# Sums of squares and gate products moved from GpSimd to VectorE, a fixed order behind the mixer's norm, and state pieces in another order, in one layer of a streaming encoder

## The chip, the cores and the metric

The kernel runs on one core of one Trainium2 chip. The metric is the device time of one execution in microseconds (us). A core has engines that run their own instruction streams beside each other: TensorE (PE, matmuls; PEld is its weight load), VectorE (DVE), ScalarE (ACT), GpSimd (POOL) and SyncE (SP), whose stream here only issues DMA transfers. A stream is carried out in order; between engines the instructions wait on semaphores. SBUF is the on-chip memory with 128 partitions, PSUM the memory into which TensorE accumulates.

## The reference

One layer of an encoder, for 256 rows of a new stream (prompt) and 32 rows of a running one (sample), 288 rows in all, that share the weights. What bears on this case:

```
xn    = rmsnorm(x, norm_mix_pre)
proj  = xn @ w_in                    # 2048 -> u_pool 1024 | z 2048 | xBC 2560 | dt 32
pool  = pool_mixer(u_pool)           # trailing means over 2/4/8/16 rows, minus u, @ w_pool, scaled
ssd   = ssd_mixer(z, xBC, dt)        # scan, times silu(z), then an rmsnorm in each of 2 groups of 1024
mix   = concat[pool, ssd] @ w_out    # 3072 -> 2048
x     = x + rmsnorm(mix, norm_mix_post)
hn    = rmsnorm(x, norm_ffn_pre)
up    = causal_dwconv(hn @ w_up)     # 2048 -> 2 x 5632
x     = x + rmsnorm((silu(gate) * value) @ w_down, norm_ffn_post)
```

with `rmsnorm(x, g) = x / sqrt(mean(x^2) + 1e-6) * g`. Besides the rows of both streams the layer returns new histories and the new scan state of each stream (`new_ssd_p`, `new_ssd_s`): for the prompt the sum over its rows of B times the decayed x, for the sample the same sum plus the decayed old state.

## The kernel before

**Layout.** Activations lie with the model's dimension on the partitions, as tiles of 128 x 288 floats. 2048 dimensions are 16 tiles (`KD`). A product with weights keeps float32 accuracy by a split: each operand is a high part (`fp32r`, made by ScalarE with a copy) and a low part (the rest, made by VectorE), and `mm3` (L135 to L138) issues three matmuls for each pair of tiles: high weight by high activation (L136), high weight by low activation (L137), low weight by high activation (L138). Weights come by DMA as `raw` tiles and are split into `whi` (L130 or L788, ScalarE) and `wlo` (L131 or L789, VectorE); `raw`, `whi` and `wlo` have 4 buffers each, so a split can run at most four ahead of TensorE. Activations are split by `split_from` (L92 to L102).

**What sets the order.** The code is written in program order, and a scheduler orders each engine's stream by its own estimate of readiness. `tc.high_priority(offset=...)` lets it take an instruction earlier. `tc.keep_in_program_order` and `tc.issue_after(x)` bind an instruction behind others of its engine. PSUM tiles come from two pools: `acc` with 5 buffers and `aux` with 3, which serves short sums (`psum_m`, `psum_t`) and further accumulators (`acc_x`).

**The stage of w_in's end and the pool mixer (L571 to L654).** `xs` are the 16 tiles of the scan's output, times silu(z). The norm of a group of 8 tiles gives a factor `rg[0]` or `rg[1]`. Tiles 0 to 7 are multiplied by `rg[0]` on VectorE earlier (L562); tiles 8 to 15 by `rg[1]` on GpSimd (L640), two for each of four turns of the loop over pool groups. That loop takes the last columns of w_in (`pool_in`), builds trailing sums `win` on VectorE (L610), forms `dpool` (L616, L617) and splits it into `du` (high part L95), which TensorE takes for w_pool. Behind it the loop over `NX` (L645) splits all `xs` into `mixs`, the inputs of w_out.

**w_out (L656 to L743).** `project` goes through 16 output tiles; for each, `mix_out` (L662) squares the result for the norm and copies it into `mg`, the `x1` tile, on ScalarE. The squares of the first 14 are summed on GpSimd into `msum`, the last two stay apart as `msq`. The mean over the partitions is three matmuls into `psum_m`: of `msum`, and of each `msq`. Between the output tiles stand four pieces of the scan state. `state_in(j)` (L681) loads `sx` (x) and `sh` (old sample state) by GpSimd's DMA queue, 2 buffers each, and decays them on VectorE (L694, L696); `state_p(j)` (L699) makes the prompt's state `pst` and `state_s(j)` (L709) the sample's `psts`, to which GpSimd adds `sh` (L716). Pieces 0 and 1 are done inside w_out, pieces 2 and 3 are held back to the end, where TensorE would wait for the norm.

**Behind the mixer's norm (L746 to L797).** `root` (L236) makes `rm`, the reciprocal root, with a ScalarE and a VectorE instruction. Then for each of 16 tiles k: VectorE multiplies `mg` by `rm` (L758) and adds the old x from `xT` (L759); ScalarE makes the high part of `hn` (L770) and VectorE the low part (L771); ScalarE squares the tile, GpSimd adds the square to `xsum` (L780); ScalarE and VectorE split the weights of this k for 7 output tiles of w_up (L788, L789); TensorE does 7 x 3 matmuls. The mean of `xsum` (`psum_t`, L797) gives the factor `r2`, by which the outputs of w_up are multiplied when they leave PSUM. From k = 2 on a weight split is bound behind both parts of `hn` of its tile.

Of the kernel before, what the change touches and what calls it, by code (L numbers as in the profile page):

```python
# [43 lines left out]
def body(  # L44
# [590 lines left out]
    for n, i in enumerate((3, 2, 1, 0)):  # L635
        ps = ups.pop() if n == 0 else project(win, [(256 * i, 256)], xn, K16)
        for j in range(2):
            pool_in(2 * i + j, ps[j])
        for t in range(8 + 2 * n, 10 + 2 * n):
            pool.tensor_tensor(xs[t], xs[t], rg[1], op=ALU.mult)  # L640
        if n:
            pool_tile(2 * i + 2)
            pool_tile(2 * i + 3)
            pool_group(i + 1)
    for t in range(NX):  # L645
        a = atile("mixs")
        split_from(a, xs[t], g_ssd[:, t : t + 1])
        mix[NU + t] = a
        if t == 3:
            pool_tile(0)  # L650
            pool_tile(1)
# [7 lines left out]
    def mix_out(p_):  # L659
        m = len(x1)  # L660
        o = btile("mg")
        if m < KD - 2:  # L662
            sq_add(msum, p_, op_, m == 0)
        else:
            q = msq[m - KD + 2]
            with tc.high_priority(offset=400):
                act.activation(q, p_, AF.Square)
            last_sq.append(q)
        if m == KD - 2:
            pe.matmul(p_m, mean, q, start=False, stop=False)  # L670
        act.activation(o, p_, AF.Copy, scale=g_mix_post[:, m : m + 1])
        x1.append(o)
# [36 lines left out]
    def state_s(j, x, h, pin=False):  # L709
# [4 lines left out]
        ho = stp[0].tile([P, 512], F32, tag="ho", bufs=2, name="hos")  # L714
        act.activation(ho, st, AF.Copy)
        pool.tensor_tensor(ho, ho, h, op=ALU.add)  # L716
        sp.dma_start(out=new_ssd_s[:, 512 * j : 512 * j + 512], in_=ho)
# [27 lines left out]

    state_s(3, *late_in[3], pin=True)  # L746
    tc.keep_in_program_order(pe.matmul(p_m, mean, last_sq[1], start=False, stop=True))
    state_p(3, *late_in[3], pin=True)
    state_s(2, *late_in[2], pin=True)
    state_p(2, *late_in[2], pin=True)  # L750
    rm = const.tile([P, NT], F32, tag="spread", bufs=3, name="rm")
    tc.keep_in_program_order(root(rm, p_m))
    hn = []
    up1 = [(aux([P, NT], "acc_x") if m in (3, 4) else acc_ps.tile([P, NT], F32, tag="acc", name="acc")) for m in range(7)]
    raws = {}

    def residual(t):
        tc.keep_in_program_order(dve.tensor_tensor(x1[t], x1[t], rm, op=ALU.mult))  # L758
        tc.keep_in_program_order(dve.tensor_tensor(x1[t], x1[t], xT[:, t, :], op=ALU.add))  # L759

    residual(0)
    for k in range(KD):
        if k % 2 == 0:
            raw = wpool.tile([P, 2, 896], F32, tag="raw", name="raw")
            with tc.high_priority(offset=ahead[0]):
                sp.dma_start(out=raw, in_=w_up1[:, k : k + 2, :])
        if k + 1 < KD:
            residual(k + 1)
        a = atile("hn")
        hi = act.activation(a[:, 0, :], x1[k], AF.Copy, scale=g_ffn_pre[:, k : k + 1])  # L770
        lo = dve.scalar_tensor_tensor(  # L771
            a[:, 1, :], x1[k], g_ffn_pre[:, k : k + 1], a[:, 0, :].bitcast(F32), op0=ALU.mult, op1=ALU.subtract
        )
        tc.keep_in_program_order(lo)
        if k == 0:
            act.activation(xsum, x1[k], AF.Square)
        else:
            q = op_.tile([P, NT], F32, tag="sq", bufs=2, name="sq")
            act.activation(q, x1[k], AF.Square)
            pool.tensor_tensor(xsum, xsum, q, op=ALU.add)  # L780
        hn.append(a)
        whi, wlo = wtile("hi", 1, 896)[:, 0, :], wtile("lo", 1, 896)[:, 0, :]
        with ExitStack() as order:
            order.enter_context(tc.high_priority(offset=ahead[0]))
            if k > 1:
# [4 lines left out]
        for m in range(7):  # L790
            c = slice(m * P, (m + 1) * P)
            mm3(up1[m], whi[:, c], wlo[:, c], a, k == 0, k == KD - 1)
            if k == KD - 1 and m == 1:
                p_ = aux([P, NT], "psum_t")
                r2 = const.tile([P, NT], F32, tag="spread", bufs=3, name="r2")
                with tc.high_priority(offset=1000):
                    pe.matmul(p_, mean, xsum, start=True, stop=True)  # L797
                    root(r2, p_)
# [39 lines left out]
    def up(kind, j, view=None):  # L838
# [4 lines left out]
        project(*((view, [(0, P)]) if view is not None else (wuv, [(kind * (D_FF - 512) + j * P - 512, 256)])), hn, K16, done=out)  # L843
# [277 lines left out]
```

## Time and profile before

| | |
|---|---|
| three runs | 1338.0, 1338.72, 1338.82 us; median 1338.72 |
| the profiled execution | 1337.7 us |
| its span | 1336.0 us |
| granted TensorE clock, mean | 0.996 |
| bytes moved by DMA | 249.82 MB |
| HBM over the span | 186 GB/s |

A row of a group reads: line of the code, engine, operation, output<-inputs, shapes, how many; busy us and mean ns of one; idle time of the engine just before and what ended it. A row of the timeline reads: start in us from the span's start, duration in us, engine, line, operation, tiles, how many together, and in brackets the idle time before it with what ended it. TensorE's instructions overlap: the starts, not the durations, tell its pace. A row of the windows reads: the stretch, its length, busy us and count for PE, PEld, DVE, ACT and POOL, then the granted TensorE clock (1.00 is full), the DMA share and GB/s.

### The profile page before, as it was taken

What the parts mean: (1) busy time and instruction counts of PE and PEld (TensorE: products, weight loads), DVE (VectorE), ACT (ScalarE), POOL (GpSimd) and SP (SyncE); (2) the same over time, 40 slices, a digit from 0 to 9 for tenths busy, and PEclk for the clock granted to TensorE, in tenths of its full rate; (3) what the DMA queues carried; (4) which work ended last, traced back from release to release, by engine and by line L of the source; (5) the groups of instructions that cost most, each with busy time, mean ns of one, the idle gap of its engine ahead of it and who ended that gap; (6) DMA issues with size and microseconds to landing.
All of it is one profiled execution on the core that took longest, in us unless ns stands there. A gap on an engine that the chain in (4) does not pass through costs nothing.

```text
span 1336.0 us, 25101 instructions
## 1 busy us (share of the span) xinstructions
PE 1312.7 (98%) x10041; PEld 1297.0 (97%) x10041; DVE 887.1 (66%) x1437; ACT 665.3 (50%) x1002; POOL 239.8 (18%) x376
## 2 busy tenths in 40 slices
PE   7999999999999999999999999999999999999996
PEld 7999999999999989999999999999999999999996
DVE  7898998788544469977676644335666666664444
ACT  7558777446443455644445433334454444454442
POOL 6221102240212123211121100001111111101110
PEclk9999999999999999999999999999999999999998
DMA  7667884456656435766544544554544544566653
GB/s 285 230 194 258 280 248 150 152 207 216 238 205 205 146 121 189 208 180 187 179 158 164 176 146 170 174 182 159 181 166 158 174 174 158 168 239 175 208 177 94
DMA packets 104009, 249.82 MB, mean 187 GB/s; under 512 B 63748, under 2 KB 69444, under 8 KB 81492
## 3 DMA queue, kind: packets, MB, share of 16 engines
q1 hardware_dynamic: 101972, 243.11, 55.4%
q0 software_dynamic: 1488, 4.92, 1.1%
q8 instruction: 78, 1.28, 0.4%
q14 instruction: 39, 0.32, 0.1%
q10 hardware_dynamic: 432, 0.19, 0.1%
HBM read 236.23 MB, written 11.95 MB: 186 GB/s over the span
## 4 chain that ended last, share of the span: by engine, by line
PE 91%; DVE 3%; DMA 2%; issue 1%; POOL 1%; ACT 0%; SPq 0%; DVEq 0%; POOLq 0%; ACTq 0%
PE acc L138 30%; PE acc L136 29%; PE acc L137 29%; DMA xw<-xs_d 1%; POOL xs L640 1%; DMA raw<-in_w_first 1%; DVE xn L100 1%; PE py L467 1%; DMA xs_d<-blocks 1%; DVE wlo L271 0%; DVE xr L959 0%; PE acc_x L138 0%; PE run_a L1002 0%; PE acc_x L137 0%; DVE wlo L131 0%
## 5 line engine op out<-in xcount | busy, mean ns | idle before, releaser
L131 DVE TENSOR_TENSOR wlo<-raw,whi 128x1024 fp32r<-128x1024 f32 (+1 forms) x386 | 464.3, 1204 | 329.4 <-ACT whi L130 328.7
L130 ACT ACTIVATE whi<-raw 128x1024 fp32r<-128x1024 f32 (+1 forms) x386 | 399.3, 1036 | 471.9 <-PE acc L137 384.9
L138 PE MATMUL acc<-hn,wlo 128*128 128x288 f32 x1376 | 409.3, 298 | 0.0
L136 PE MATMUL acc<-hn,whi 128*128 128x288 f32 x1376 | 402.5, 293 | 0.5 <-ACT hn L770 0.5
L137 PE MATMUL acc<-hn,whi 128*128 128x288 f32 x1376 | 399.6, 291 | 1.2 <-DVE hn L771 1.2
L137 PEld LDWEIGHTS acc<-hn,whi 128*128 128x128 f32 x1376 | 258.9, 188 | 1.5 <-DVE hn L771 1.4
L136 PEld LDWEIGHTS acc<-hn,whi 128*128 128x128 f32 x1376 | 258.7, 188 | 1.3 <-ACT hn L770 1.3
L138 PEld LDWEIGHTS acc<-hn,wlo 128*128 128x128 f32 x1376 | 258.7, 188 | 0.0
L136 PE MATMUL acc<-xn,whi 128*128 128x288 f32 x688 | 203.8, 298 | 5.6 <-ACT whi L270 5.6
L137 PE MATMUL acc<-xn,whi 128*128 128x288 f32 x688 | 200.8, 293 | 0.0
L138 PE MATMUL acc<-xn,wlo 128*128 128x288 f32 x688 | 198.7, 298 | 1.6 <-DVE wlo L271 1.4
L138 PE MATMUL acc<-fa,wlo 128*128 128x288 f32 x660 | 196.4, 298 | 0.0
L136 PE MATMUL acc<-fa,whi 128*128 128x288 f32 x660 | 193.1, 293 | 0.0
L137 PE MATMUL acc<-fa,whi 128*128 128x288 f32 x660 | 191.4, 290 | 0.0
L136 PEld LDWEIGHTS acc<-xn,whi 128*128 128x128 f32 x688 | 130.3, 189 | 6.5 <-ACT whi L270 5.6
L137 PEld LDWEIGHTS acc<-xn,whi 128*128 128x128 f32 x688 | 130.3, 189 | 0.2
L138 PEld LDWEIGHTS acc<-xn,wlo 128*128 128x128 f32 x688 | 127.7, 189 | 2.6 <-DVE wlo L271 1.6
L137 PEld LDWEIGHTS acc<-fa,whi 128*128 128x128 f32 x660 | 123.9, 188 | 0.0
L136 PEld LDWEIGHTS acc<-fa,whi 128*128 128x128 f32 x660 | 123.9, 188 | 0.0
L138 PEld LDWEIGHTS acc<-fa,wlo 128*128 128x128 f32 x660 | 123.9, 188 | 0.0
L816 POOL COPY fc_stage<-ebuf 128x4 f32<-128x4 f32 x88 | 27.2, 309 | 466.8 <-DVE ebuf L815 466.8
L812 POOL COPY ebuf<-pf 128x2 f32<-128x2 f32 x88 | 67.4, 767 | 140.6 <-DVE fc L822 79.4
(279 smaller groups left out, 1716.1 us busy)
## 6 DMA issues: line engine op xcount, KB each, us to landing
raw<-in_w_up SPq DMA_DIRECT2D x80, 1024.0 KB, 4.8
raw<-in_w_in SPq DMA_DIRECT2D x38, 1024.0 KB, 5.4
raw<-in_w_down SPq DMA_DIRECT2D x32, 1024.0 KB, 4.8
raw<-in_w_out SPq DMA_DIRECT2D x24, 1024.0 KB, 4.8
raw<-in_w_down SPq DMA_DIRECT2D x16, 768.0 KB, 4.3
raw<-in_w_up SPq DMA_DIRECT2D x8, 896.0 KB, 4.5
gb<-g_d SPq DMA_DIRECT2D x8, 832.0 KB, 6.6
raw<-in_w_first SPq DMA_DIRECT2D x7, 768.0 KB, 10.2
```

Source lines behind the costliest of these rows:

```text
L100: dve.scalar_tensor_tensor(a[:, 1, :], src, scale, a[:, 0, :].bitcast(F32), op0=ALU.mult, op1=ALU.subtract),
L130: act.activation(hi, raw[:, k : k + n, :], AF.Copy)
L131: dve.tensor_tensor(lo, raw[:, k : k + n, :], hi.bitcast(F32), op=ALU.subtract)
L136: pe.matmul(out, wh, a[:, 0, :], start=start, stop=False)
L137: pe.matmul(out, wh, a[:, 1, :], start=False, stop=False)
L138: pe.matmul(out, wl, a[:, 0, :], start=False, stop=stop)
L467: pe.matmul(y[:, 0:256], xw[:, 0, c], m[:, j, 0:256], start=True, stop=False)
L640: pool.tensor_tensor(xs[t], xs[t], rg[1], op=ALU.mult)
L812: pool.tensor_copy(e[:, 258:260], pf[:, 4:6, i])
L816: pool.tensor_copy(fc_stage[:, :, :, i], e[:, 256:324].rearrange("p (s c) -> p s c", c=34)[:, :, 0:2])
```

## The change

It has five parts.

1. The products of `xs` 8 to 15 with `rg[1]` move from GpSimd (L640) to VectorE, into the loop that splits `xs`; each stands behind the low part of the tile before it.
2. Both matmuls of `msq` into `psum_m` are issued together right behind the last matmul of w_out, then both sample pieces and then both prompt pieces of the state. Before, the first was issued in `mix_out`, and the order behind it was sample piece 3, last sum, prompt 3, sample 2, prompt 2.
3. `in_line` binds VectorE's instructions behind the norm (product, addition, low part, sum of squares) each to the one before it, in program order. The product and addition of tile k + 1 stand ahead of the low part of tile k. The sum of squares moves from GpSimd to this line. Weight splits are bound behind `hn` from k = 4 on, not from k = 2.
4. `psum_t` is allocated ahead of the 7 accumulators, in the buffer that follows `psum_m`'s in turn, its matmul is bound in place (in the last tile, behind the second of 7 outputs), and the product of w_up that comes next takes its accumulator from the `aux` pool (`spare=1`).
5. `state_s` copies the sum into `sx`, and GpSimd adds it into `sh`, which is written out; the tile `hos` goes.

```diff
--- before.py
+++ after.py
@@ -636,15 +636,16 @@
         ps = ups.pop() if n == 0 else project(win, [(256 * i, 256)], xn, K16)
         for j in range(2):
             pool_in(2 * i + j, ps[j])
-        for t in range(8 + 2 * n, 10 + 2 * n):
-            pool.tensor_tensor(xs[t], xs[t], rg[1], op=ALU.mult)
         if n:
             pool_tile(2 * i + 2)
             pool_tile(2 * i + 3)
             pool_group(i + 1)
     for t in range(NX):
         a = atile("mixs")
-        split_from(a, xs[t], g_ssd[:, t : t + 1])
+        if t >= 8:
+            with tc.issue_after(low.ins):
+                dve.tensor_tensor(xs[t], xs[t], rg[1], op=ALU.mult)
+        _, low = split_from(a, xs[t], g_ssd[:, t : t + 1])
         mix[NU + t] = a
         if t == 3:
             pool_tile(0)
@@ -666,8 +667,6 @@
             with tc.high_priority(offset=400):
                 act.activation(q, p_, AF.Square)
             last_sq.append(q)
-        if m == KD - 2:
-            pe.matmul(p_m, mean, q, start=False, stop=False)
         act.activation(o, p_, AF.Copy, scale=g_mix_post[:, m : m + 1])
         x1.append(o)
 
@@ -711,10 +710,9 @@
         ins = pe.matmul(st, btok[:, j // 2, 2, :], x[:, 2, :], start=True, stop=True)
         if pin:
             tc.keep_in_program_order(ins)
-        ho = stp[0].tile([P, 512], F32, tag="ho", bufs=2, name="hos")
-        act.activation(ho, st, AF.Copy)
-        pool.tensor_tensor(ho, ho, h, op=ALU.add)
-        sp.dma_start(out=new_ssd_s[:, 512 * j : 512 * j + 512], in_=ho)
+        act.activation(x[:, 2, :], st, AF.Copy)
+        pool.tensor_tensor(h, h, x[:, 2, :], op=ALU.add)
+        sp.dma_start(out=new_ssd_s[:, 512 * j : 512 * j + 512], in_=h)
 
     late_in = {}
 
@@ -743,20 +741,32 @@
             act.dma_start(out=new_pool, in_=np_stage)
 
 
+    for i in range(2):
+        tc.keep_in_program_order(pe.matmul(p_m, mean, last_sq[i], start=False, stop=i == 1))
     state_s(3, *late_in[3], pin=True)
-    tc.keep_in_program_order(pe.matmul(p_m, mean, last_sq[1], start=False, stop=True))
+    state_s(2, *late_in[2], pin=True)
     state_p(3, *late_in[3], pin=True)
-    state_s(2, *late_in[2], pin=True)
     state_p(2, *late_in[2], pin=True)
     rm = const.tile([P, NT], F32, tag="spread", bufs=3, name="rm")
-    tc.keep_in_program_order(root(rm, p_m))
+    root(rm, p_m)
+    out_temp = lambda: op_.tile([P, NT], F32, tag="sq", bufs=2, name="sq")
     hn = []
+    p_t = aux([P, NT], "psum_t")
     up1 = [(aux([P, NT], "acc_x") if m in (3, 4) else acc_ps.tile([P, NT], F32, tag="acc", name="acc")) for m in range(7)]
     raws = {}
 
+    line = []
+
+    def in_line(f, *args, **kw):
+        with ExitStack() as order:
+            if line:
+                order.enter_context(tc.issue_after(line[-1].ins))
+            line.append(f(*args, **kw))
+        return line[-1]
+
     def residual(t):
-        tc.keep_in_program_order(dve.tensor_tensor(x1[t], x1[t], rm, op=ALU.mult))
-        tc.keep_in_program_order(dve.tensor_tensor(x1[t], x1[t], xT[:, t, :], op=ALU.add))
+        in_line(dve.tensor_tensor, x1[t], x1[t], rm, op=ALU.mult)
+        in_line(dve.tensor_tensor, x1[t], x1[t], xT[:, t, :], op=ALU.add)
 
     residual(0)
     for k in range(KD):
@@ -764,25 +774,25 @@
             raw = wpool.tile([P, 2, 896], F32, tag="raw", name="raw")
             with tc.high_priority(offset=ahead[0]):
                 sp.dma_start(out=raw, in_=w_up1[:, k : k + 2, :])
+        a = atile("hn")
+        hi = act.activation(a[:, 0, :], x1[k], AF.Copy, scale=g_ffn_pre[:, k : k + 1])
         if k + 1 < KD:
             residual(k + 1)
-        a = atile("hn")
-        hi = act.activation(a[:, 0, :], x1[k], AF.Copy, scale=g_ffn_pre[:, k : k + 1])
-        lo = dve.scalar_tensor_tensor(
-            a[:, 1, :], x1[k], g_ffn_pre[:, k : k + 1], a[:, 0, :].bitcast(F32), op0=ALU.mult, op1=ALU.subtract
+        lo = in_line(
+            dve.scalar_tensor_tensor,
+            a[:, 1, :], x1[k], g_ffn_pre[:, k : k + 1], a[:, 0, :].bitcast(F32), op0=ALU.mult, op1=ALU.subtract,
         )
-        tc.keep_in_program_order(lo)
         if k == 0:
             act.activation(xsum, x1[k], AF.Square)
         else:
-            q = op_.tile([P, NT], F32, tag="sq", bufs=2, name="sq")
+            q = out_temp()
             act.activation(q, x1[k], AF.Square)
-            pool.tensor_tensor(xsum, xsum, q, op=ALU.add)
+            in_line(dve.tensor_tensor, xsum, xsum, q, op=ALU.add)
         hn.append(a)
         whi, wlo = wtile("hi", 1, 896)[:, 0, :], wtile("lo", 1, 896)[:, 0, :]
         with ExitStack() as order:
             order.enter_context(tc.high_priority(offset=ahead[0]))
-            if k > 1:
+            if k > 3:
                 order.enter_context(tc.issue_after(hi.ins))
                 order.enter_context(tc.issue_after(lo.ins))
             act.activation(whi, raw[:, k % 2, :], AF.Copy)
@@ -791,11 +801,10 @@
             c = slice(m * P, (m + 1) * P)
             mm3(up1[m], whi[:, c], wlo[:, c], a, k == 0, k == KD - 1)
             if k == KD - 1 and m == 1:
-                p_ = aux([P, NT], "psum_t")
                 r2 = const.tile([P, NT], F32, tag="spread", bufs=3, name="r2")
                 with tc.high_priority(offset=1000):
-                    pe.matmul(p_, mean, xsum, start=True, stop=True)
-                    root(r2, p_)
+                    tc.keep_in_program_order(pe.matmul(p_t, mean, xsum, start=True, stop=True))
+                    root(r2, p_t)
     x1d = dram.tile([NT, D_MODEL], F32, name="x1d")
     outp.close()
 
@@ -840,7 +849,10 @@
         def out(m, p_):
             conv_[kind, j + m] = fconv(kind * NF + j + m, p_)
 
-        project(*((view, [(0, P)]) if view is not None else (wuv, [(kind * (D_FF - 512) + j * P - 512, 256)])), hn, K16, done=out)
+        if view is not None:
+            project(view, [(0, P)], hn, K16, done=out, spare=1)
+        else:
+            project(wuv, [(kind * (D_FF - 512) + j * P - 512, 256)], hn, K16, done=out)
 
     def up_half(lo_, hi_):
         for j in range(lo_, hi_, 2):
```

How the instructions move is shown at three places. First, GpSimd in the stage of the pool mixer, both kernels in one piece (`ubuf` are the pool inputs, `np_stage` the new pool history):

```order
 L604 COPY np_stage<-ubuf_3587 128x30
 L604 COPY np_stage<-ubuf_3589 128x30
-L640 TENSOR_TENSOR xs<-xs,rg 128x288 x7
 L599 COPY ubuf_3587<-pc 128x15
-L640 TENSOR_TENSOR xs<-xs,rg 128x288
 L599 COPY ubuf_3589<-pc 128x15
 L604 COPY np_stage<-ubuf_3591 128x30
```

The eight products are gone, and the copies into the `ubuf` tiles follow each other. On VectorE, in the same stage, the first of them stand here (`du` low part of a pool input, `mixs` low part of an `xs` tile):

```order
 L131 TENSOR_TENSOR wlo<-raw,whi 128x1024
 L100 TENSOR_SCALAR mixs<-xs,g_ssd,mixs 128x288
+L647 TENSOR_TENSOR xs<-xs,rg 128x288
 L96 TENSOR_TENSOR du<-dpool,du 128x288
-L100 TENSOR_SCALAR mixs<-xs,g_ssd,mixs 128x288 x3
 L131 TENSOR_TENSOR wlo<-raw,whi 128x1024
 L597 TENSOR_TENSOR ubuf_3591<-acc,rstd 128x256
 L598 TENSOR_TENSOR ubuf_3591<-acc,rstd 128x32
-L100 TENSOR_SCALAR mixs<-xs,g_ssd,mixs 128x288 x3
+L100 TENSOR_SCALAR mixs<-xs,g_ssd,mixs 128x288
+L647 TENSOR_TENSOR xs<-xs,rg 128x288
```

The products stand one by one ahead of the low parts of their tiles, behind the low part of the tile before.

Second, ScalarE at the end of w_out, before (`msq` squares of the last two outputs, `whi` weight splits, L788 those of w_up, `rm` the root, `ho` and `hos` copies of the state):

```order
L788 ACTIVATE whi<-raw 128x896 x2
L667 ACTIVATE msq_3581<-acc 128x288
L671 ACTIVATE mg<-acc,par_119 128x288
L667 ACTIVATE msq_3582<-acc 128x288
L671 ACTIVATE mg<-acc,par_119 128x288
L715 ACTIVATE hos<-psts 128x512
L237 ACTIVATE rm<-psum_m,eps_t 128x288
L706 ACTIVATE ho<-pst 128x512
L715 ACTIVATE hos<-psts 128x512
L770 ACTIVATE hn<-mg,par_119 128x288
L776 ACTIVATE xsum<-mg 128x288
L706 ACTIVATE ho<-pst 128x512
```

and now:

```order
L798 ACTIVATE whi<-raw 128x896 x3
L668 ACTIVATE msq_3581<-acc 128x288
L670 ACTIVATE mg<-acc,par_119 128x288
L798 ACTIVATE whi<-raw 128x896
L668 ACTIVATE msq_3582<-acc 128x288
L670 ACTIVATE mg<-acc,par_119 128x288
L237 ACTIVATE rm<-psum_m,eps_t 128x288
L713 ACTIVATE sx<-psts 128x512 x2
L705 ACTIVATE ho<-pst 128x512
L778 ACTIVATE hn<-mg,par_119 128x288
L786 ACTIVATE xsum<-mg 128x288
L778 ACTIVATE hn<-mg,par_119 128x288
```

One weight split more stands ahead of the squares, one between them, and the root comes before all copies of the state.

Third, VectorE behind the reciprocal, before (`mg` the products and additions, `hn` low parts, `wlo` weight splits):

```order
L789 TENSOR_TENSOR wlo<-raw,whi 128x896 x2
L238 RECIPROCAL rm<-rm 128x288
L758 TENSOR_TENSOR mg<-mg,rm 128x288 x3
L759 TENSOR_TENSOR mg<-mg,xT_3578 128x288
L758 TENSOR_TENSOR mg<-mg,rm 128x288
L759 TENSOR_TENSOR mg<-mg,xT_3578 128x288 x3
L771 TENSOR_SCALAR hn<-mg,par_119,hn 128x288 x3
L789 TENSOR_TENSOR wlo<-raw,whi 128x896
L758 TENSOR_TENSOR mg<-mg,rm 128x288
L759 TENSOR_TENSOR mg<-mg,xT_3578 128x288
```

and now (all instructions of the line carry the line number of `in_line`'s call, L764):

```order
L799 TENSOR_TENSOR wlo<-raw,whi 128x896 x4
L238 RECIPROCAL rm<-rm 128x288
L764 TENSOR_TENSOR mg<-mg,rm 128x288
L764 TENSOR_TENSOR mg<-mg,xT_3578 128x288
L764 TENSOR_TENSOR mg<-mg,rm 128x288
L764 TENSOR_TENSOR mg<-mg,xT_3578 128x288
L764 TENSOR_SCALAR hn<-mg,par_119,hn 128x288
L764 TENSOR_TENSOR mg<-mg,rm 128x288
L764 TENSOR_TENSOR mg<-mg,xT_3578 128x288
L764 TENSOR_SCALAR hn<-mg,par_119,hn 128x288
L764 TENSOR_TENSOR xsum<-xsum,sq 128x288
L764 TENSOR_TENSOR mg<-mg,rm 128x288
```

The first low part of `hn` moves from the ninth place behind the reciprocal to the fifth, and the sums `xsum` enter the line.

## The prediction

> **What bounds the kernel now.** I read the page first, then TensorE's own table of waits, then the places in time where those waits stand. From the page: the span, the busy time by engine, and the chain that ended last.
>
> ```profile
> span 1336.0 us, 25101 instructions
> ...
> PE 1312.7 (98%) x10041; PEld 1297.0 (97%) x10041; DVE 887.1 (66%) x1437; ACT 665.3 (50%) x1002; POOL 239.8 (18%) x376
> ...
> PE 91%; DVE 3%; DMA 2%; issue 1%; POOL 1%; ACT 0%; SPq 0%; DVEq 0%; POOLq 0%; ACTq 0%
> ```
>
> TensorE works 98% of the span and carries 91% of the chain, and the change takes no matmul away. So it can gain only where TensorE stands still, or runs slowly. The table of TensorE's waits (total us, times, longest) names where it stands still; four of its rows lie where the change works:
>
> ```profile
> PE psum_t L797 <- POOL xsum L780: 2.2, 1, 2.2
> PE acc L136 <- ACT du L95: 1.9, 1, 1.9
> ...
> PE acc L137 <- DVE hn L771: 1.2, 1, 1.2
> PE acc L136 <- ACT hn L770: 0.5, 1, 0.5
> ```
>
> Together 5.8 us: that is the size of what can be won by waits. The profiled execution took 1337.7 us (span and 1.7 us around it), 1.0 us under the median of 1338.72; I make the sum against 1337.7 and add 1.0 at the end.
>
> **Part 1: eight products of `xs` leave GpSimd for VectorE.** Rows of the timeline (start, duration), VectorE's older products of the same shape first (smallest/median/largest ns):
>
> ```profile
> L562 DVE TENSOR_TENSOR xs<-xs,rg x8: 447/449/450, 229.7 to 232.3; 128x288 f32<-128x288 f32 x8
> ...
> L640 POOL TENSOR_TENSOR xs<-xs,rg 128x288 f32<-128x288 f32 x8 | 9.0, 1150 | 1.6 <-DVE rg L238 1.6
> ...
> 280.71 3.10 DVE L610 TENSOR_TENSOR win<-win 128x315 f32<-128x315 f32 x3
> 287.70 1.01 DVE L616 SCALAR_TENSOR_TENSOR dpool<-win,ubuf 128x256 f32<-128x256 f32 x1
> 294.00 0.47 DVE L610 TENSOR_TENSOR win<-win 128x315 f32<-128x315 f32 x1
> 296.13 0.41 DVE L616 SCALAR_TENSOR_TENSOR dpool<-win,ubuf 128x256 f32<-128x256 f32 x1
> ...
> 288.80 0.44 ACT L95 ACTIVATE du<-dpool 128x288 fp32r<-128x288 f32 x1 [3.60 <-POOL ubuf L599]
> ...
> 287.08 0.29 PE L138 MATMUL acc<-xn,wlo 128*128 128x288 f32 x1
> 289.29 0.54 PE L136 MATMUL acc<-du,whi 128*128 128x288 f32 x2 [1.92 <-ACT du L95]
> ```
>
> GpSimd's run of eight lasts from 279.3 to 288.4. Inside it VectorE's `win` additions take 1.03 us each (3.10/3) and the last `dpool` 1.01; outside it the same forms take 0.47 and 0.41. So the run delays `dpool`, ScalarE's `du` behind it starts at 288.80, and TensorE, which issues a matmul every 0.13 us, starts the next one 2.21 us after the last: 2.08 us lost. Without the run, the four additions and the `dpool` of these rows save 4 x 0.56 + 0.60, about 2.8 us ahead of `du` at least (a fourth `win` from 283.73 is stretched likewise). `du` then starts at 286.0 or sooner and is there at 286.4, before it is needed at 287.21. What the move costs: 8 x 0.45 = 3.6 us more on VectorE, placed behind the first `dpool` of this stage, between the splits of `xs`. Against the 2.8 saved that is 0.8 us later for VectorE, and TensorE comes 2.1 sooner; the matmuls that follow hide it, since the table has no wait on `mixs` in that stage, and replaying the rows with the moved products leaves the last splits of `xs` about 3 us ahead of their use. If that cover went, a wait at `mixs` of the amount exceeded would stand there. Term: -2.1 (bounds -2.1 and, if another late tile takes `du`'s place at once, 0).
>
> [...]
>
> **Part 2: the mixer's norm and the start of the line.** TensorE, ScalarE, VectorE and GpSimd around it:
>
> ```profile
> 477.74 1.02 PE L711 MATMUL psts<-sx,btok 128*128 128x512 f32 x2
> 479.08 0.65 PE L747 MATMUL psum_m<-msq,mean 128*128 128x288 f32 x2
> 479.57 1.88 PE L702 MATMUL pst<-sx,btok 128*128 128x512 f32 x4
> 484.47 0.67 PE L136 MATMUL acc<-hn,whi 128*128 128x288 f32 x3 [0.45 <-ACT hn L770]
> 486.89 0.40 PE L137 MATMUL acc<-hn,whi 128*128 128x288 f32 x1 [1.20 <-DVE hn L771]
> ...
> 477.94 0.41 ACT L667 ACTIVATE msq<-acc 128x288 f32<-128x288 f32 x1 [0.77 <-PE acc L138]
> 487.64 0.94 ACT L788 ACTIVATE whi<-raw 128x896 fp32r<-128x896 f32 x1
> ...
> 480.30 1.95 DVE L238 RECIPROCAL rm<-rm 128x288 f32<-128x288 f32 x1 [6.71 <-ACT rm L237]
> 483.77 1.53 DVE L758 TENSOR_TENSOR mg<-mg,rm 128x288 f32<-128x288 f32 x1
> 486.33 0.51 DVE L771 SCALAR_TENSOR_TENSOR hn<-mg,par,hn 128x288 fp32r<-128x288 f32 x1
> ...
> 483.56 1.43 POOL L716 TENSOR_TENSOR hos<-hos,sh 128x512 f32<-128x512 f32 x1 [2.82 <-ACT hos L715]
> ```
>
> The norm's sum is now ahead of all four state pieces on TensorE, but a weight split (0.94 us as at 487.64) stands on ScalarE ahead of the last square. That square moves from 477.94 to about 478.65, so the second sum starts near 479.11, as before (479.08), and TensorE idles 0.9 us at 478.2 where a state piece ran. The reciprocal stays at 480.3; the state pieces (two of 0.86, two of 1.71) end at 484.74. So the first `hn` matmul moves 0.27 us later than its 484.47. The gain is behind it: VectorE did three products, an addition, a product under GpSimd's addition (1.53 us) and three more additions before the first low part at 486.33. Bound link by link the first low part is the fifth link: 482.29 + 4 x 0.45 = 484.1 and ready at 484.6; with both GpSimd additions (1.3 to 1.4 us each, now near 481.2 and 482.5) holding one link for the whole of the second one, 485.6. TensorE's eighth matmul, which read it at 486.89, would go at 484.74 + 7 x 0.131 = 485.66 or, at the latest of these, 486.0. Gain 0.9 to 1.2; I take 1.1. Bounds: -1.7 (both waits gone, nothing added) and +0.3 (only the later start counts).
>
> **Part 3: the squares' sum leaves GpSimd and joins the line.** The span from the first product to the end of the `psum_t` wait (us, then busy us of the engines with counts, clock), then the rows of one tile of 16:
>
> ```profile
> 482.20:525.20 43.00, 39.16 (x285) 37.41 (x283) 42.04 (x62) 27.07 (x49) 17.95 (x16) 1.00 0.39 129
> ...
> L780 POOL TENSOR_TENSOR xsum<-xsum,sq 128x288 f32<-128x288 f32 x15 | 16.5, 1102 | 23.5 <-ACT sq L779 23.5
> ...
> 497.34 0.51 DVE L771 SCALAR_TENSOR_TENSOR hn<-mg,par,hn 128x288 fp32r<-128x288 f32 x1
> 497.77 1.08 DVE L789 TENSOR_TENSOR wlo<-raw,whi 128x896 fp32r<-128x896 f32 x1
> 498.77 0.45 DVE L758 TENSOR_TENSOR mg<-mg,rm 128x288 f32<-128x288 f32 x1
> 499.25 0.46 DVE L759 TENSOR_TENSOR mg<-mg,xT 128x288 f32<-128x288 f32 x1
> 499.63 1.06 DVE L771 SCALAR_TENSOR_TENSOR hn<-mg,par,hn 128x288 fp32r<-128x288 f32 x1
> ```
>
> VectorE was full here: 42.04 of 43.00 us for 62 instructions, 0.678 us each, because in every tile one of its links fell under a GpSimd addition (1.06 instead of 0.51). GpSimd's 15 go away, VectorE gets 15 of about 0.45. The new line has 16 products, 16 additions, 16 low parts, 15 sums and 12 weight splits (four splits now run ahead): 75 links, 16 x 0.45 + 16 x 0.46 + 16 x 0.51 + 15 x 0.45 + 12 x 1.08 = 42.4 us by the rows' durations; by starts (0.43, 1.00, 0.48, 0.38 between the five rows, 0.45 for the sum) 2.74 a tile with a split, about 40. From 482.3 it ends between 522 and 525. TensorE needs 21 matmuls a tile, 2.75 us, so the two keep the same pace and the four early splits leave VectorE some 3 to 5 us ahead. The wait itself:
>
> ```profile
> 522.63 0.29 PE L138 MATMUL acc<-hn,wlo 128*128 128x288 f32 x1
> 525.12 0.75 PE L797 MATMUL psum_t<-xsum,mean 128*128 128x288 f32 x2 [2.19 <-POOL xsum L780]
> ...
> 526.63:529.98 3.35, 3.35 (x17) 3.35 (x15) 3.35 (x4) 1.06 (x1) 0.00 (x0) 0.50 0.79 249
> ```
>
> TensorE lost 2.49 - 0.13 = 2.36 us. In the changed order `psum_t` stands 42 matmuls later (5.5 us), at about 484.74 + 321 x 0.131 = 526.8, behind the line's end: the wait goes, -2.4 (bounds -2.4 and the price of rival C). What is late next is the root and its reciprocal for the first evacuations of the up-projection; with `psum_t` in a tile allocated earlier and one more buffer lent to the next product, I find 3 us between them and their use.
>
> The last row adds a term. For 3.35 us, beginning 1.1 us after `psum_t` ran, the granted clock was 0.50, where over the 43 us before it was 1.00. That is 3.35 x 0.5 = 1.7 us at most; 14 matmuls start in it where 0.131 us each makes 1.8 of the 3.35, so 1.5. I take it to be a consequence of the wait, and that it goes with it: -1.5 (bounds -1.7 and 0).
>
> [...]
>
> **Part 4: the state pieces add into the loaded tile.** The copy of the sum goes into `sx`, the addition into `sh`, which is written out. So the next loads into these tiles wait for GpSimd's addition and for the output's landing. Issue rows (KB, us to landing) and a row of TensorE:
>
> ```profile
> sh<-in_state_ssd POOLq DMA_DIRECT2D x4, 256.0 KB, 6.6
> ...
> out<-hos SPq DMA_DIRECT2D x4, 256.0 KB, 4.4
> ...
> 399.15 1.45 PE L702 MATMUL pst<-sx,btok 128*128 128x512 f32 x3
> ```
>
> `sx` comes about 2.6 us later; `sh` is issued after the landing: 383.4 + 4.4 + 6.6 = 394.4. The weight splits queued behind it on VectorE follow at about 396; the first of them is used by TensorE only behind the pieces at 399.15, near 399.8. Cover 3.7 us here and 3 the second time: nothing.
>
> **Sum.** -2.1 - 1.1 - 2.4 - 1.5 = -7.1: 1337.7 becomes 1330.6, and with the 1.0 of the median 1331.6.
>
> **Rivals.** [...] A: GpSimd's two additions hold links of the line's start, 0.3 lost instead of 1.1 gained: 1333.0; for it speaks the 1.53 us at 483.77. D: `du` is replaced by another late tile, since VectorE's rows there follow one another without idle time: 1333.7. C, on the other side: VectorE's line, now with the sums and in fixed order, is the bound. If a link kept the 0.678 us of before, because each waits for ScalarE's square or high part, 75 links end at 482.3 + 50.9 = 533.2, TensorE waits 6.4 us, and with the clock's loss back the total is -2.1 - 1.1 - 2.4 + 6.4 = +0.8: 1339.5, no change. From 0.71 us a link (end at 535.6, wait 8.8) it is slower by over 0.2%, at 0.75 (538.6) 1344.9. For it speaks only that VectorE is 98% full there; against it, that the stretched links all coincide with GpSimd's additions.
>
> **How the numbers follow.** 0.2%, 2.7 us, is about what a measurement of this kernel can tell from no change. Forecast 0.50, B 0.16, A 0.09, D 0.07: these are faster, 0.82. C at the old pace 0.10, same; C beyond 0.71 us a link, or a load of part 4 later than its cover by far more, 0.08, slower. The likeliest is 1331.6, by itself 1330.4 to 1333. The range goes down to 1329.8 (the mixer's bound of -1.7 and its neighbours) and up to 1337.0: the faster cases and the near end of C.
>
> **What would show it.** Right: no wait of TensorE on `du`, `hn`'s low part or `xsum` in its table; `win` additions of 0.47 at 281; 75 links from 482 to 525 with GpSimd empty beside them; clock 1.00 from 520 to 535; a new idle of 0.9 us ahead of the second norm sum. Wrong: a wait at `psum_t` or at an `hn` or `wlo` of the line, `mixs` late, a split behind `sh` late, or a stretch at 0.50.

## The result and the profile after

The changed kernel takes 1330.14 us (median of 4 runs, 1329.62 to 1330.5) against 1338.36 us before (4 runs, 1337.66 to 1338.82): a ratio of 0.9944, 95% interval 0.9932 to 0.9957. That is 8.2 us, where 7.1 were forecast. The profiled execution took 1329.91 us, its span 1328.2. From its page, span, busy time and the chain that ended last:

```profile
span 1328.2 us, 25077 instructions
...
PE 1310.4 (99%) x10041; PEld 1295.1 (98%) x10041; DVE 884.6 (67%) x1460; ACT 666.3 (50%) x1002; POOL 215.0 (16%) x353
...
PE 98%; DVE 1%; DMA 0%; ACT 0%; issue 0%; DVEq 0%; SPq 0%
```

TensorE's waits (total us, times, longest) are now:

```profile
PE acc L136 <- ACT whi L270: 5.7, 1, 5.7
PE acc L138 <- DVE wlo L271: 1.3, 1, 1.3
PE psum_f L931 <- ACT fsq L960: 0.8, 1, 0.8
PE psum_m L745 <- ACT msq L668: 0.7, 1, 0.7
```

All four waits that the prediction quoted are gone from the table, and the one that it announced is there, 0.7 us ahead of the second norm sum. TensorE's busy time fell by 2.3 us too, with the same number of matmuls; the half clock, 1.5 us of it by the starts, is gone (1.00 where 0.50 was granted). First the stage of the pool mixer, on the timeline of the changed kernel:

```profile
279.60 1.53 DVE L610 TENSOR_TENSOR win<-win 128x315 f32<-128x315 f32 x3
283.38 0.41 DVE L616 SCALAR_TENSOR_TENSOR dpool<-win,ubuf 128x256 f32<-128x256 f32 x1
...
284.62 0.42 ACT L95 ACTIVATE du<-dpool 128x288 fp32r<-128x288 f32 x1
...
286.74 0.43 PE L136 MATMUL acc<-du,whi 128*128 128x288 f32 x2
```

Three `win` additions take 1.53 us instead of 3.10, `du` is made at 284.62 and lies ready 1.7 us before its use. Then the mixer's norm:

```profile
475.08 0.29 PE L138 MATMUL acc<-mixp,wlo 128*128 128x288 f32 x1
475.21 0.65 PE L745 MATMUL psum_m<-msq,mean 128*128 128x288 f32 x2
476.58 0.75 PE L745 MATMUL psum_m<-msq,mean 128*128 128x288 f32 x2 [0.72 <-ACT msq L668]
482.55 0.67 PE L136 MATMUL acc<-hn,whi 128*128 128x288 f32 x3
483.58 0.30 PE L138 MATMUL acc<-hn,wlo 128*128 128x288 f32 x1
...
478.90 2.71 POOL L714 TENSOR_TENSOR sh<-sh,sx 128x512 f32<-128x512 f32 x2 [20.01 <-ACT sx L713]
...
480.52 1.41 DVE L764 TENSOR_TENSOR mg<-mg,xT 128x288 f32<-128x288 f32 x1
482.70 0.51 DVE L764 SCALAR_TENSOR_TENSOR hn<-mg,par,hn 128x288 fp32r<-128x288 f32 x1
...
482.55 0.43 PEld L136 LDWEIGHTS acc<-hn,whi 128*128 128x128 f32 x3 [0.89 <-ACT hn L778]
```

The first addition of the line is stretched from 0.46 to 1.41 us under GpSimd's two additions; ScalarE's first `hn` comes that much later, and the weight load for the first `hn` matmul waits 0.89 us for it. This wait isn't in TensorE's table, because a part of it lies under the last state piece. Last the line itself and the place of the half clock, in windows (us, busy us with counts for PE, PEld, DVE, ACT, POOL, then clock):

```profile
479.89:519.29 39.40, 39.33 (x286) 37.55 (x285) 38.85 (x75) 25.66 (x47) 1.72 (x2) 1.00 0.41 142
526.63:529.98 3.35, 3.35 (x28) 3.35 (x27) 3.35 (x4) 1.07 (x1) 0.00 (x0) 1.00 0.67 210
...
524.92 0.65 PE L806 MATMUL psum_t<-xsum,mean 128*128 128x288 f32 x2
```

The 75 links take 39.4 us, 0.525 each, and end 5.6 us ahead of `psum_t`. Where 17 matmuls ran at half clock, 28 run.

The difference of the two traces, read at matmuls of the same number from the start (before minus after): 0.47 us ahead of the first `du` matmul (287.08 and 286.61), where the program is the same; 2.52 at the last matmul of w_out (477.60 and 475.08); 3.31 at the eighth `hn` matmul (486.89 and 483.58) and 3.41 from the ninth on; still 3.40 at the last matmul ahead of the old `psum_t` (522.63 and 519.23); 7.36 once `psum_t` and the half clock are past, up to the last matmul; 7.8 at the end. So the three places are worth 2.05, 0.88 (0.79 at the eighth matmul) and 3.96.

### The profile page after: what moved, and what is told of

The parts are those of the page before. It is cut to its first block, busy times and chain, and to the rows that moved or that the text cites. A ratio compares the mean times of both kernels' runs of the same rounds, so it can differ in the third digit from the quotient of the medians.

```text
span 1328.2 us, 25077 instructions
## 1 busy us (share of the span) xinstructions
PE 1310.4 (99%) x10041; PEld 1295.1 (98%) x10041; DVE 884.6 (67%) x1460; ACT 666.3 (50%) x1002; POOL 215.0 (16%) x353
## 4 chain that ended last, share of the span: by engine, by line
PE 98%; DVE 1%; DMA 0%; ACT 0%; issue 0%; DVEq 0%; SPq 0%
PE acc L138 31%; PE acc L136 31%; PE acc L137 31%; PE acc_x L138 1%; PE acc_x L137 1%; PE acc_x L136 1%; PE py L467 1%; DVE xr L971 0%; PE run_a L1014 0%; PE low L1012 0%; DMA raw<-in_w_first 0%; PE py L469 0%; PE pst L701 0%; PE run_b L1027 0%; PE pdt L289 0%; DVE mg L764 0%
## 5 line engine op out<-in xcount | busy, mean ns | idle before, releaser
L138 PE MATMUL acc<-hn,wlo 128*128 128x288 f32 x1360 | 397.7, 293 | 0.0
L136 PEld LDWEIGHTS acc<-hn,whi 128*128 128x128 f32 x1360 | 255.3, 188 | 0.9 <-ACT hn L778 0.9
L137 PEld LDWEIGHTS acc<-hn,whi 128*128 128x128 f32 x1360 | 255.3, 188 | 0.1
L138 PEld LDWEIGHTS acc<-hn,wlo 128*128 128x128 f32 x1360 | 255.2, 188 | 0.0
L138 PE MATMUL acc<-fa,wlo 128*128 128x288 f32 x660 | 193.1, 293 | 0.0
L831 DVE SCALAR_TENSOR_TENSOR fc<-ebuf,pf,fc 128x290 f32<-128x290 f32 x176 | 90.2, 518 | 2.9 <-ACT fc L829 0.3
## 6 DMA issues: line engine op xcount, KB each, us to landing
raw<-in_w_first SPq DMA_DIRECT2D x7, 768.0 KB, 10.1
```

The source lines that it names most:

```text
L136: pe.matmul(out, wh, a[:, 0, :], start=start, stop=False)
L137: pe.matmul(out, wh, a[:, 1, :], start=False, stop=False)
L138: pe.matmul(out, wl, a[:, 0, :], start=False, stop=stop)
L831: dve.scalar_tensor_tensor(c, e[:, r_ : r_ + 290], pf[:, r_, i : i + 1], c, op0=ALU.mult, op1=ALU.add)
```

## The experiments

All were made from the changed kernel. The runs of the kernel before scattered by 4 to 5 us in these series, so differences of under 1 us are read at the same matmul of two traces, relative to a place ahead of the edit. The changed kernel itself, once more:

> The changed kernel once more, unaltered, beside the others on one chip. Expected: 7 to 8 us under the kernel before, no half clock between 480 and 540, and the same three waits of TensorE as in its first profile besides the second norm sum.

1330.07 us (5 runs, 1329.5 to 1330.46), ratio to before 0.994, interval 0.9926 to 0.9954. The clock was 1.00 throughout that stretch, 0.998 in the mean of the run. Two waits came and went with chance (0.7 us at an early `py`, some tenths on early splits): ahead of the first changed place this trace runs 0.20 us behind the other one of the same kernel. The fourteen traces of this case reach that matmul, with the same program for TensorE up to there, between 286.43 and 289.05 us. So the 0.47 us of difference there, and as much of the 8.2, is scatter.

**The products of `xs` back on GpSimd.**

```diff
+        for t in range(8 + 2 * n, 10 + 2 * n):
+            pool.tensor_tensor(xs[t], xs[t], rg[1], op=ALU.mult)
...
-        if t >= 8:
-            with tc.issue_after(low.ins):
-                dve.tensor_tensor(xs[t], xs[t], rg[1], op=ALU.mult)
...
```

> The changed kernel with the eight products of xs back on GpSimd. Theory (GpSimd's run delays the last dpool, and the du wait is all of its price): a wait of TensorE on du of about 2 us comes back at 287, 1330.1 + 2.1 = 1332.2, and nothing else changes. Rival (the products were paid for elsewhere by VectorE, or another late tile stands behind du): under 1 us, 1330.1 to 1331.

1333.07 us (1332.27 to 1333.32). TensorE's row is back, and at this place the trace falls back by 2.1 us (from 0.97 to 3.05 behind the first trace of the changed kernel):

```profile
287.58 0.29 PE L138 MATMUL acc<-xn,wlo 128*128 128x288 f32 x1
289.79 0.40 PE L136 MATMUL acc<-du,whi 128*128 128x288 f32 x1 [1.92 <-ACT du L95]
...
288.00:290.00 2.00, 0.21 (x1) 0.21 (x2) 1.97 (x4) 0.70 (x2) 1.27 (x2) 1.00 0.25 107
290.00:292.00 2.00, 2.00 (x16) 2.00 (x16) 2.00 (x6) 0.69 (x1) 0.00 (x0) 1.00 0.00 0
```

Behind this place nothing moved by more than 0.2 us. GpSimd's run is the whole of this term. No half clock followed this wait of 1.92 us: the granted clock was 1.00 from 286 to 296.

**The sums of squares back on GpSimd.**

```diff
-            in_line(dve.tensor_tensor, xsum, xsum, q, op=ALU.add)
+            pool.tensor_tensor(xsum, xsum, q, op=ALU.add)
```

> The changed kernel with the sums of squares back on GpSimd; the line of the other links and the late place of psum_t stay. Theory (either of the two moves alone, the sum to VectorE or psum_t 42 matmuls later, takes away most of the psum_t wait): the last wlo of the line near 524.0 and the last sum near 524.2, against TensorE at 523.9 and 524.9, so a loss of 0 to 0.6 us, 1330.1 to 1330.7, and no stretch at half clock. Rival (GpSimd's additions themselves are the cost, wherever psum_t stands): a psum_t wait of 2 us or more and half clock behind it, 1332 to 1334.

1331.41 us (1330.44 to 1332.84). The trace is 2.44 us behind already ahead of the edit and 2.60 behind after it: the edit costs 0.2 us. There is no wait at `psum_t`:

```profile
482.50:527.00 44.50, 44.43 (x323) 42.63 (x322) 43.60 (x62) 27.18 (x49) 19.73 (x17) 1.00 0.40 137
...
518.50 1.06 DVE L764 TENSOR_TENSOR mg<-mg,xT 128x288 f32<-128x288 f32 x1
521.90 2.08 DVE L799 TENSOR_TENSOR wlo<-raw,whi 128x896 fp32r<-128x896 f32 x2
...
520.61 1.05 POOL L790 TENSOR_TENSOR xsum<-xsum,sq 128x288 f32<-128x288 f32 x1 [1.36 <-ACT sq L789]
...
527.54 0.65 PE L806 MATMUL psum_t<-xsum,mean 128*128 128x288 f32 x2
```

The links are stretched as before (62 instructions in 43.60 us), yet the last sum is ready at 521.66, 5.9 us ahead of `psum_t`. Even 42 matmuls earlier (5.5 us) it would just have been in time. So the sum's move was not needed to end the wait and, by these times, neither was the late place of `psum_t`, each taken by itself. That leaves the rest of the line's change (order, splits ahead), which brought the last sum forward far enough; this is concluded from what is left, and no run takes out the order and the splits one at a time.

**Without the binding link by link.**

```diff
-            if line:
-                order.enter_context(tc.issue_after(line[-1].ins))
```

> The changed kernel without the binding link by link; all else stays, and the order of VectorE behind the reciprocal is the scheduler's: 8 products, an addition, 4 products, an addition, 2 products, 6 additions, a product, and then the first low part. Theory (the place of the first low part in VectorE's stream is what the start behind the norm hangs on): the first low part comes at about 479.9 + 23 x 0.4 = 489.1 and TensorE's L137 at 489.6 instead of 483.45, so 5 to 6 us slower, 1335 to 1336. Rival (the line is free to be late as TensorE has other matmuls to do): under 2 us slower.

1338.83 us (10 runs), ratio to before 1.0011, interval 1.0002 to 1.002: the whole gain is gone. TensorE's table has two new waits:

```profile
PE acc L137 <- DVE hn L762: 3.8, 1, 3.8
PE acc L136 <- ACT hn L776: 2.6, 1, 2.6
...
481.20 4.25 DVE L762 TENSOR_TENSOR mg<-mg,rm 128x288 f32<-128x288 f32 x8
490.90 0.51 DVE L762 SCALAR_TENSOR_TENSOR hn<-mg,par,hn 128x288 fp32r<-128x288 f32 x1
```

At the same matmul the trace falls back by 8.3 us here, more than the 5 to 6 expected: 2.6 at the first high part and 4.0 at the low part, about what its place gives, and 1.7 by a half clock of 6.8 us, which the expectation had left out. This order is the scheduler's own, with the first low part in place 24 behind the reciprocal; in the kernel before it stood ninth. So the 8.3 us are the price of leaving the line unbound, and not what the change won at this place.

**One link more in each tile.**

```diff
             in_line(dve.tensor_tensor, xsum, xsum, q, op=ALU.add)
+            in_line(dve.tensor_tensor, xsum, xsum, xsum, op=ALU.max)
```

> One link more (0.45 us) in each of 15 tiles of VectorE's line, which does not alter the sum. Theory (the line is ahead of TensorE: its end at 519.3 against psum_t at 524.9, 5.6 us, of which 6.8 us are now used): 15 x 0.45 = 6.8 us more, so a loss of 0.5 to 2.5 us, 1330.6 to 1332.6, seen as waits on hn or wlo late in the line. Rival (the line already bounds TensorE): nearly all 6.8 us are lost, 1336 to 1337.

1338.01 us (1336.88 to 1339.9), ratio to before 1.0008, interval 0.9999 to 1.0018. By the number the rival wins; the trace says otherwise. Up to the last two tiles TensorE doesn't wait on the line: no matmul starts more than 0.14 us after the one before. The trace still goes from 0.18 us ahead at the start of the stage to 0.33 behind near its end, mostly because the mean step is 0.133 instead of 0.131 us. (The scheduler also ordered the matmuls of a tile in another way here; whether that sets the pace wasn't tried.) What is late by more is the sum alone:

```profile
PE psum_t L807 <- DVE xsum L764: 3.6, 1, 3.6
...
524.57 1.08 DVE L800 TENSOR_TENSOR wlo<-raw,whi 128x896 fp32r<-128x896 f32 x1
525.57 2.36 DVE L131 TENSOR_TENSOR wlo<-raw,whi 128x1024 fp32r<-128x1024 f32 x2
527.84 0.46 DVE L764 TENSOR_TENSOR xsum<-xsum,sq 128x288 f32<-128x288 f32 x1
528.21 2.36 DVE L131 TENSOR_TENSOR wlo<-raw,whi 128x1024 fp32r<-128x1024 f32 x2
530.48 0.46 DVE L764 TENSOR_TENSOR xsum<-xsum 128x288 f32<-128x288 f32 x1
```

The scheduler set four weight splits of the next product (4.5 us) between the last links. Without them the last link would end near 526.4, before TensorE asks for it at 527.3. So the line had room for nearly all of the 6.8 us, and what cost 7.4 us was the tail: a wait of 3.6, one of 0.6 for the root behind it, and half clock for 6.8.

**A wait at `psum_t` of chosen length.** The additions add zero.

```diff
+    pool.memset(msum, 0.0)
...
+                for _ in range(9):
+                    pool.tensor_tensor(xsum, xsum, msum, op=ALU.add)
```

> Nine idle additions on GpSimd (0.8 us each) stand between the finished sum and psum_t, to make a wait like that of before without GpSimd beside the line. Theory (the half clock follows such a wait): a psum_t wait of 1 to 2 us, and behind it a stretch of some 3.4 us at half clock: loss of the wait and 1.5 us more. Rival (the half clock has nothing to do with the wait): loss of the wait alone, granted clock 1.00.

> The same with twelve additions: a psum_t wait of about 4 us. Theory: the wait and 1.5 us more, with half clock behind it. Rival: the wait alone. If the clock falls here and not with nine, the length of the wait decides.

> Seven idle additions (1.26 us each as the run with nine showed) ahead of psum_t: a wait of about 1.4 us and 0.6 us behind it for the root. Theory (a wait of over about 2 us is followed by half clock, a shorter one not): granted clock 1.00 throughout, loss of 2 to 2.5 us, 1332.1 to 1332.6. Rival (any wait there brings it): half clock for some us and 3.5 us or more lost.

1337.93 us with nine, 1340.42 with twelve, 1332.33 with seven (range(7)). The waits were 3.8, 6.4 and 1.1 us, each followed by 0.6 for the root; the scheduler had also put `psum_t` 15 matmuls further on than in the changed kernel. Windows of the runs with seven, nine and twelve, in this order:

```profile
528.00:530.00 2.00, 1.07 (x4) 0.62 (x5) 1.79 (x3) 0.68 (x2) 0.28 (x1) 1.00 0.12 49
530.00:532.00 2.00, 2.00 (x17) 2.00 (x16) 1.97 (x2) 0.00 (x0) 0.00 (x0) 1.00 0.82 176
```

```profile
532.00:534.00 2.00, 2.00 (x8) 2.00 (x9) 1.97 (x2) 0.00 (x0) 0.00 (x0) 0.50 0.93 301
534.00:536.00 2.00, 2.00 (x13) 2.00 (x12) 2.00 (x9) 1.35 (x3) 0.75 (x4) 0.69 0.14 22
536.00:538.00 2.00, 2.00 (x17) 2.00 (x16) 2.00 (x6) 1.98 (x4) 0.27 (x2) 1.00 0.05 9
```

```profile
534.00:536.00 2.00, 1.41 (x4) 0.58 (x4) 0.92 (x2) 0.50 (x1) 0.00 (x0) 0.50 0.00 0
538.00:540.00 2.00, 2.00 (x10) 2.00 (x9) 2.00 (x9) 1.77 (x4) 0.77 (x4) 0.50 0.06 10
540.00:542.00 2.00, 2.00 (x17) 2.00 (x16) 2.00 (x6) 1.46 (x2) 0.34 (x1) 0.99 0.33 55
```

With seven no half clock, and 2.3 us lost at this place, which by the starts is the two waits. With nine half clock for 3.4 us and 6.4 us lost, 1.5 more than the waits' 4.9; with twelve for 10.2 us, part of it during the wait, and 10.1 lost. So here the half clock is a consequence of the wait: it came with waits of 3.8 and 6.4 us, and not with that of 1.1.

**State pieces.** One sample piece between the two sums again, as before the change:

```diff
-    for i in range(2):
-        tc.keep_in_program_order(pe.matmul(p_m, mean, last_sq[i], start=False, stop=i == 1))
-    state_s(3, *late_in[3], pin=True)
-    state_s(2, *late_in[2], pin=True)
-    state_p(3, *late_in[3], pin=True)
+    tc.keep_in_program_order(pe.matmul(p_m, mean, last_sq[0], start=False, stop=False))
+    state_s(3, *late_in[3], pin=True)
+    tc.keep_in_program_order(pe.matmul(p_m, mean, last_sq[1], start=False, stop=True))
+    state_p(3, *late_in[3], pin=True)
+    state_s(2, *late_in[2], pin=True)
```

> One sample piece of the state is put back between the two norm sums, as before the change. Theory (the start behind the norm is set by the chain second square, norm sum, root, reciprocal, line, and not by TensorE's pieces): TensorE's 0.7 us of idle time is filled and turns up as a wait on hn instead, 1330.1 within 0.3. Rival (the order of the pieces carried the gain at the mixer's norm): about 0.8 us faster with the idle time filled, or about 0.6 us slower.

1331.24 us (1330.17 to 1331.72). The 0.7 us of idle time ahead of the second sum are filled, and a wait of 0.7 on the first low part of `hn` has come instead (and one of 0.2 on a weight split). At the same matmul: 1.09 behind ahead of the edit, level at the first `hn` matmul, 1.01 behind at the eighth, 1.29 behind after the stage. GpSimd's second addition now falls on the third link:

```profile
481.47 0.46 DVE L764 TENSOR_TENSOR mg<-mg,xT 128x288 f32<-128x288 f32 x1
481.85 1.53 DVE L764 TENSOR_TENSOR mg<-mg,rm 128x288 f32<-128x288 f32 x1
483.42 0.46 DVE L764 TENSOR_TENSOR mg<-mg,xT 128x288 f32<-128x288 f32 x1
483.79 0.51 DVE L764 SCALAR_TENSOR_TENSOR hn<-mg,par,hn 128x288 fp32r<-128x288 f32 x1
```

So the first addition is short and the first `hn` matmul 1.1 us sooner, but the first low part starts 7.6 us behind the last matmul of w_out in both traces. The order of the pieces carried no gain. And with the tile `hos` of before:

```diff
-        act.activation(x[:, 2, :], st, AF.Copy)
-        pool.tensor_tensor(h, h, x[:, 2, :], op=ALU.add)
+        ho = stp[0].tile([P, 512], F32, tag="ho", bufs=2, name="hos")
+        act.activation(ho, st, AF.Copy)
+        pool.tensor_tensor(ho, ho, h, op=ALU.add)
```

> The changed kernel with the sample pieces of the state as before: copied into a tile of their own, GpSimd's addition there, sh free at once. Theory (part 4 of the prediction: later loads are covered): the same time within 0.4 us, the loads of sx about 2 us and of sh about 5 to 7 us earlier, and no wait of TensorE gone or new. Rival: a wait on a split behind sh shows that the cover was used, a gain of 0.5 us or more.

1330.24 us (1329.72 to 1331.3), no wait gone or new in these stages, the trace 0.1 to 0.2 us ahead of the changed kernel's from the edit on, as ahead of it. The load of `sh` is issued at 381.00 instead of 385.62, and VectorE uses it at 389.71 instead of 389.19. In the changed kernel VectorE idles 0.35 us for the later load, which costs nothing here.

**Three splits ahead instead of four.**

```diff
-            if k > 3:
+            if k > 2:
```

> Three weight splits run ahead instead of four, so no split stands between the last two squares of the mixer's norm on ScalarE. Theory (that split delays the second norm sum by 0.85 us, and with it the reciprocal, the line and the first hn matmul): the idle 0.7 us of TensorE ahead of the second sum goes, the first hn matmul comes about 0.9 us sooner, 1329.2; the one split more in the line (1.1 us) is covered. Rival (the line has no room for it): a wait on wlo or hn takes the gain back, 1330.1 or more.

1330.32 us (1330.03 to 1331.56). The 0.7 us ahead of the second norm sum are gone and the first `hn` matmul comes 0.71 us sooner (0.37 behind ahead of it, 0.34 ahead behind it). 0.3 is given back in small steps along the line, and the rest and more at `psum_t`, to 0.57 behind: the scheduler's order of the last matmuls put it 13 places further on, so the root comes late, and TensorE waits 0.3 us for it. The same with the matmuls of the last two tiles bound in program order:

```diff
-            mm3(up1[m], whi[:, c], wlo[:, c], a, k == 0, k == KD - 1)
+            if k < KD - 2:
+                mm3(up1[m], whi[:, c], wlo[:, c], a, k == 0, False)
+            else:
+                for w_, j in ((whi, 0), (whi, 1), (wlo, 0)):
+                    tc.keep_in_program_order(
+                        pe.matmul(up1[m], w_[:, c], a[:, j, :], start=False, stop=k == KD - 1 and w_ is wlo)
+                    )
```

> Three splits ahead instead of four, as in the run with that edit, and the matmuls of the last two tiles bound in program order, so that psum_t does not slip behind 13 others. Theory (that run won 0.85 us at the mixer's norm and lost it again to a psum_t that came 2 us later, with TensorE waiting for the root): 0.8 us under the changed kernel, with no wait for a root behind psum_t. Rival (the fifth split in the line costs it): 0.3 us or less under it, or slower.

1329.83 us (5 runs, 1329.72 to 1330.27), ratio to before 0.9939, interval 0.9924 to 0.9955. The wait for the root is gone. At the same matmul 0.71 us are won at the norm and 0.3 given back along the line; 0.4 stay. Beside the changed kernel's 1330.07 that is no difference that these runs can tell. The small steps are no waits: as in the run with one link more, no step is over 0.14 us, but the mean is 0.1326 instead of 0.1313. What sets that pace was not found.

## Why the prediction was right, point by point

**Part 1, the `du` wait: right.** -2.1 forecast, 2.05 in the traces, 2.1 when undone. The stretched `win` and `dpool` were the cause, and the 3.6 us more on VectorE stayed covered.

**Part 2, the mixer's norm: right in its mechanism, too large by 0.2 to 0.3.** -1.1 forecast (0.9 to 1.2), 0.79 measured at the eighth matmul and 0.88 from the ninth on. The second sum came 1.50 us behind the last matmul of w_out, as worked out (479.11 - 477.60). The step that was off is "So the first `hn` matmul moves 0.27 us later than its 484.47": it moved 0.60 later. Not the state pieces set it but ScalarE's `hn`, behind the addition that GpSimd stretched by 0.95 us. That is rival A's mechanism, in part: the prediction let it delay the low part, but not the high part ahead of it. The run with a sample piece between the sums bears this out: with a first addition of 0.46 us ScalarE's first `hn` and the first matmul came 1.1 us sooner. That run also shows that the order of the pieces isn't what the gain hangs on, and the run without the binding that the place of the first low part in the line is.

The hold of a link under GpSimd's additions, 1.0 us in the later of the two estimates (484.6 against 485.6), was 0.95: the line's first addition took 1.41 us beside them and 0.46 in the run with a sample piece between the sums.

**Part 3, the wait at `psum_t`: right in amount, its reason too narrow.** The wait and the half clock together were forecast at -3.9 and are 3.96. "From 482.3 it ends between 522 and 525", about 40 to 43 us: measured 39.4. The prediction put the end of the wait on the sum's move and on the later place; the run with the sum on GpSimd shows that the move could go without the wait coming back, and by its times the place could too, which no run tried. VectorE's line was not the bound, and rival C falls: stretched by 6.8 us it still kept ahead of TensorE up to the sum itself, which the scheduler then made late. How much of the gain the order has and how much the splits ahead isn't shown; three ahead did as well as four.

**The half clock: right.** -1.5 forecast as a consequence of the wait; the runs with a wait of chosen length show it. The chance of 0.16 for B stood for a clock that falls even when the wait is gone, and no run shows that: behind `psum_t` the clock was 1.00 in the changed kernel, with no wait there, and with seven additions, with one of 1.1 us. In the kernel before, 3.4 us at half clock came 1.5 us behind a wait of 2.2.

**Part 4, the loads: right, with a price of nothing.** The estimate of 394.4 for `sh` was 2.7 us too late: the load was issued when the sum said (385.62, in a trace that runs 2.5 us ahead of that of before), but VectorE used it 3.6 us later, where 6.6 had been put in from the median of the kernel before.

**The sum.** -7.1 against 8.2 by the medians and 7.8 between the two profiled executions. The three places give 6.9 in the traces; 0.5 lies ahead of the change, where traces of the same program differ by up to 2.6, and 0.4 behind the last matmul. So the missing microsecond is not a part that was overlooked, as far as these runs can tell.

## What to carry to other kernels

Where a reduction closes a stage, look at which instruction stands first in the in-order stream behind it: leaving the first tile's links unbound, behind those of other tiles, cost 8 us here, the half clock included, more than any work moved back. When several edits aim at one wait, undo them one at a time: here the move of the sums could be undone without the wait. And a wait on TensorE cost more than its length here where the clock fell with it: two short waits (1.1 and 0.6 us, 2.3 lost) were cheaper than one of 2.2 (2.4 lost, and 1.5 more by the clock).

## What the runs showed of the hardware that was not expected

The stretches at half clock lasted 3.4 us (before, nine additions), 6.8 (one link more, no binding) and 10.2 (twelve additions). A matmul started every 0.24 us in that of before (526.63 to 529.98), and every 0.13 ahead of it. TensorE's waits, and the moment at which the clock fell, in us from the span's start:

| run | wait (us), its end | the clock falls | half clock |
|---|---|---|---|
| before, at `psum_t` | 2.2, 525.1 | 526.6, behind the wait | 3.4 |
| nine additions | 3.8, 530.7; 0.6, 532.0 | 531.8, in the second | 3.4 |
| one link more | 3.6, 531.0; 0.6, 532.9 | 530.6, in the first | 6.8 |
| twelve additions | 6.4, 533.7; 0.6, 535.6 | 529.8, in the first | 10.2 |
| no binding | 2.6, 486.4; 3.8, 491.5 | 488.4, in the second | 6.8 |
| seven additions | 1.1 and 0.6 | not | 0 |
| before, at `du` | 1.9, 289.3 | not | 0 |
| products on GpSimd, at `du` | 1.9, 289.8 | not | 0 |

From the beginning of the first wait of a row to the fall it took 2.5 us (twelve additions) to 5.0 (nine). In the run without the binding the clock was still 1.00 while TensorE worked for 1.2 us behind its wait of 2.6, and fell 0.8 us into the next one:

```profile
486.00:487.00 1.00, 0.56 (x4) 0.56 (x5) 1.00 (x4) 0.72 (x2) 0.00 (x0) 1.00 0.02 4
487.00:488.00 1.00, 0.63 (x5) 0.40 (x4) 1.00 (x4) 0.30 (x1) 0.00 (x0) 1.00 0.00 0
488.00:489.00 1.00, 0.00 (x0) 0.00 (x0) 1.00 (x4) 0.76 (x3) 0.00 (x0) 0.70 0.00 0
489.00:490.00 1.00, 0.00 (x0) 0.00 (x0) 1.00 (x4) 1.00 (x4) 0.00 (x0) 0.50 0.00 0
...
494.00:495.00 1.00, 1.00 (x6) 1.00 (x6) 1.00 (x4) 0.73 (x3) 0.00 (x0) 0.50 0.00 0
495.00:496.00 1.00, 1.00 (x8) 1.00 (x8) 1.00 (x3) 1.00 (x2) 0.00 (x0) 0.89 0.00 0
```

The rows whose longest wait was 1.1 or 1.9 us have no half clock, those with 2.2 to 6.4 us have it. But the length of the wait gives neither the moment of the fall nor the length of the stretch: a wait of 3.8 us came with 3.4 at half clock, one of 3.6 with 6.8. What sets them was not shown.
